# A decoder layer with expert retrieval on one core: steps traced later, the last gate's rows in their own buffers, and a final norm without GpSimd

## The chip, the cores and the metric

The kernel runs on one core of one Trainium2 chip. A core has a matrix engine (TensorE: PE in the profile, with PEld for its weight loads), a vector engine (VectorE: DVE), a scalar engine (ScalarE: ACT), GpSimd (POOL) and SyncE (SP). Each engine takes its own instructions strictly in the order in which they were issued, and waits at the head of its queue until the semaphores of that instruction are there. Transfers are issued from the queues of SP, ACT and POOL. The metric is device time in microseconds (us).

## What is computed

One decoder layer on 256 tokens of width 1024, in float32: a modulated norm, one input projection that feeds sparse attention and a short convolution, an output projection, a second modulated norm, an expert layer with 16384 experts of which each token picks 16 in each of 8 heads, and a final norm. The expert layer takes most of the time:

```python
def peer_ffn(xn, w_q, sub_keys, expert_u, expert_v):
    q = (xn @ w_q).reshape(B, S, PEER_HEADS, 2, PEER_QDIM // 2)
    s = jnp.einsum('bshpd,hpkd->bshpk', q, sub_keys)
    v_half, i_half = lax.top_k(s, PEER_TOPK)
    cand = v_half[..., 0, :, None] + v_half[..., 1, None, :]
    top_s, top_c = lax.top_k(cand.reshape(B, S, PEER_HEADS, PEER_TOPK * PEER_TOPK), PEER_TOPK)
    ...
    experts = i1 * PEER_NKEYS + i2
    g = jax.nn.softmax(top_s.astype(jnp.float32), axis=-1)
    ...
        u = expert_u[ec]
        act = jax.nn.gelu(jnp.einsum('cd,ced->ce', xc, u).astype(jnp.float32))
        return jnp.einsum('ce,ced->cd', gc * act, expert_v[ec])
# and in the layer: x = x + gt2 * peer_ffn(h2, ...); return rmsnorm(x, ln_final_g)
```

## The kernel before

The front part (norm, attention, convolution, output projection, second norm) ends at about 206 us of the span and is not touched. What follows is traced by hand: from L720 on the program is in manual order, so an engine's queue holds its instructions in the order in which the Python code traces them, and to "trace a step later" is to move it back in the queue of every engine that it uses.

**The first product.** All 128 tiles of `expert_u` (a tile is 128 experts x 1024) are multiplied with the 256 tokens. A weight tile is loaded on SP's queue into a ring of four buffers (`wraw`), ACT casts it to a high part (`whi`, L118), and the low part (`wlo`, L119) is a subtraction on GpSimd for tiles below `XL` and on VectorE from there on. `ahead` keeps three split tiles ready; `u_tile(i)` then issues 24 matmuls of 256 columns. ACT follows with the gelu.

- Tiles 0 to 27 (`XA` = 28, L1052): beside them VectorE finds the top experts (`topk`, a generator; each `yield` names an estimated cost, and a tile lets 2.2 us of it be traced). Its last step makes `keys` (L1007 to L1017), which TensorE transposes into `keyT` (L1066). The eight tiles of `w_mod` for the last gate go through the same `wraw` ring, one after every third u tile, and `last_gate` (L1030) adds each to `acc5` on VectorE.
- Tiles 28 to 61 (`XG` = 62, L1156): beside them the dense gate matrix is built: `gate.onehots` (VectorE, from `keyT`) and `gate.products` (16 short matmuls for 8 tokens).
- Tiles 62 to 127 (L1369): `make_list` finds which experts of which half of the tokens are used (`find_used`, 16 steps), numbers them, and in `list_part` makes two lists of row numbers, 8 columns at a time: three operations on VectorE (`oneR`, `oneQ`, half of `oneT`), one on ACT (the other half of `oneT`, L1215), and 8 short matmuls, which are traced one chunk later. A tile lets 2.7 of the estimated cost be traced. Products are stored to memory (`rows`) by SP. As soon as the first list is there, `pick` gathers activation rows with an indirect transfer from GpSimd's queue, up to 48 of them (`NA`) before the loop ends. At tile 100 (`XM`) `gate_rows` makes the last gate's rows: two scalings on VectorE, matmuls, additions, all traced at once.

**The second product** (L1438). For each of 95 listed columns of 128 experts, GpSimd gathers a tile of `expert_v` (128 x 1024) and, if it wasn't done before, the activation rows; `split_acts` (L1407) splits the activations (`ah` on ACT, `al` on VectorE), `next_weights` splits a weight tile two columns ahead, and TensorE adds 12 matmuls of 512 columns (both halves of the tokens) or 6 (one half). In ACT's and VectorE's queues the split of the activations of column n+1 stands behind the split of the weights of column n+2. There are as many v tiles in flight as seven buffers allow, and `pick` is called at a rate of 0.6 for each column until all 95 are picked.

**The end** (`tail`, L1511): residual, mean of squares, norm and output; GpSimd multiplies three halves of rows by the norm's gain.

Of the kernel before, what the change touches and what calls it, by code (L numbers as in the profile page):

```python
# [30 lines left out]
XL = 92  # L31
# [25 lines left out]
def layer(nc, tc, d, dbg=None):  # L57
# [37 lines left out]
    def mod_tile(j, k):  # L95
        return d["w_mod"][k * 128:(k + 1) * 128, j * D:(j + 1) * D]
# [769 lines left out]
    nmod = [0]  # L866
# [45 lines left out]
    def topk():  # L912
# [94 lines left out]
        ei = k.tile([128, 3, T], I32, name="ei")  # L1007
        V.tensor_copy(ei[:, 0], eid.rearrange("p t j -> p (t j)"))
        V.tensor_scalar(ei[:, 1], ei[:, 0], 7, None, op0=OP.logical_shift_right)
        V.tensor_scalar(ei[:, 2], ei[:, 0], 127, None, op0=OP.bitwise_and)  # L1010
        two = lambda ap: ap.unsqueeze(2).to_broadcast([128, T, 2])
        for n in range(2):
            V.tensor_copy(keys[:, n], two(ei[:, 1 + n]))
        ws = k.tile([128, T], F32, name="ws")
# [13 lines left out]
    acc5 = k.tile([128, D], F32, name="acc5")  # L1028

    def last_gate(raw):  # L1030
        gather_mod(acc5, raw, nmod[0])
        nmod[0] += 1
        if nmod[0] == KT_:
            Q.dma_start(acc5d, acc5)
# [8 lines left out]
    steps = topk()  # L1043
    for h, _ in enumerate(queries()):
        if h == H:
            S.activation(Ba[:, 0], u_tile(0), AF.Gelu_apprx_tanh)
        if h > 1:
            next(steps)
            next(steps)
            next(steps)  # L1050
    show("sco", sco)
    for i in range(1, XA):  # L1052
        S.activation(Ba[:, i], u_tile(i), AF.Gelu_apprx_tanh)  # L1053
        credit[0] += FREE
        while credit[0] > 0:
            credit[0] -= next(steps, 9.0)
# [3 lines left out]
    bs.close()  # L1060
    kt = pool("pskey", space=PSUM, stack=us)
# [140 lines left out]
    def list_part(p, work, pl, e1, e0, e, q0, n):  # L1202


        last = None
        for c0 in list(range(e0, e, 8)) + [None]:
            if c0 is not None:
                w = min(8, e - c0)
                cs = slice(c0, c0 + w)
                r = work.tile([128, 8, 128], F16, name="oneR", bufs=2)  # L1210
                paired(r[:, :w], io1, w, pl[0][:, cs], OP.is_equal)
                q = work.tile([128, 8, n], F16, name="oneQ%d" % n, tag="oneQ", bufs=1)
                paired(q[:, :w], io1[:, q0:q0 + n], w, pl[1][:, cs], OP.is_equal)
                t = work.tile([128, 8, 2, n], F16, name="oneT%d" % n, tag="oneT", bufs=2)
# [3 lines left out]
            if last:  # L1218
                l0, lw_, r0, t0 = last
                for c in range(lw_):  # L1220
                    mm(p, r0[:, c], t0[:, c].rearrange("p k q -> p (k q)"), l0 + c == e0, l0 + c == e - 1)
            last = c0 is not None and (c0, w, r, t)
# [10 lines left out]
    def make_list():  # L1233
# [21 lines left out]
        cs = lw.tile([NL, 3, 128], F16, name="cs")  # L1255
# [12 lines left out]
        t = lw.tile([128, 3, NL], F32, name="t3", tag="t3")  # L1268
        V.tensor_tensor(t, pos, m, op=OP.mult)
        un = lw.tile([128, NL], F32, name="un")  # L1270
# [6 lines left out]
        pi = lw.tile([128, 3, NL], I32, name="pi", tag="t3")  # L1277
# [36 lines left out]
    def gate_rows(acc5, out):  # L1314

        V.tensor_scalar(out, out, 1.0 / GSC, None, op0=OP.mult)
        V.tensor_scalar(acc5, acc5, 1.0 / GSC, None, op0=OP.mult)
        for n in range(2):
            cs = slice(n * 512, n * 512 + 512)
            p = keyT[n].rearrange("p a t -> p (a t)")  # L1320
            mm(p, ones, acc5[:, cs], True, True)
            V.tensor_add(out[:, cs], p, out[:, cs])
# [45 lines left out]
    log = []  # L1368
    for i in range(XG, NE):  # L1369
        gelu_tile(i)  # L1370
# [7 lines left out]
        if i == XM:  # L1378
            gate_rows(acc5, g2)
# [3 lines left out]
        credit[0] += 2.7  # L1383
# [7 lines left out]
    print("picks from", log[:1], "picked", len(picked), "stored", stored[0], "lists", ready_lists)  # L1391
# [3 lines left out]
    settle()  # L1395
    store_rows(NL)
# [31 lines left out]

    for i in range(NL, NE):
        acts = split_acts(Bb[:, i - XA], slice(0, T))  # L1430
        w = next_weights()
        for a in range(2):
            out_tile(acts, w, a)
# [4 lines left out]
    for n, q in enumerate(taken):  # L1438
        while later and len(taken) - len(later) < n0 + 2 + (n + 1) * 6 // 10:
            pick()  # L1440
        if n == 40:
            Q.dma_start(x1, x1d)
            row_bias(2, lnf)
            S.preload_act_table_set("natural_log_exp_and_others")
        t, halves = picked.pop(q), halves_of(q)
        acts = split_acts(t, columns(halves))
# [64 lines left out]
    def tail(fin):  # L1511
# [6 lines left out]
        G.tensor_mul(y[:, 0, 512:], x1[:, 0, 512:], lnf[:, 512:])  # L1518
# [6 lines left out]
        G.tensor_mul(y[:, 1, :512], x1[:, 1, :512], lnf[:, :512])  # L1525
# [17 lines left out]
        S.activation(y[:, 0, 512:], y[:, 0, 512:], AF.Copy, scale=r0)  # L1543
        store(0, Q, 512, 1024)
# [88 lines left out]
```

## Time and profile before

| | us |
|---|---|
| three runs before | 940.42, 942.26, 935.8 (median 940.42) |
| the profiled execution's own time | 935.07 |
| its span, first to last instruction | 933.1 |
| TensorE busy | 844.1 |
| VectorE busy | 672.2 |
| ScalarE busy | 471.7 |
| GpSimd busy | 514.8 |

The difference of 2.0 us between the execution's time and its span lies around the program. Busy times overlap. A row of the timeline gives the start, the duration, the engine and the line, and in brackets how long the engine had been idle and what ended that. A group of a view by line gives the busy time and the mean of one. The granted clock is TensorE's, as a share of its full speed.

### The profile page before, as it was taken

To read this page: it belongs to the slowest core of one execution; us is meant where nothing else is said; L and a number is where in the kernel's file an instruction comes from. 1 tells how busy PE (TensorE), PEld (TensorE's weight loads), DVE (VectorE), ACT (ScalarE), POOL (GpSimd) and SP (SyncE) were. 2 spreads that over 40 slices of the span, in tenths; PEclk is the share of its full clock that TensorE was granted. 3 is DMA by queue.
4 is the path that set the end of the run, shared out by engine and by line. 5 is a ranking of instruction groups with operands and counts; after the bars stand their busy time and mean duration, and the time that the engine had idled before them with its cause. 6 is when DMAs were issued, how large, how long until landed. Compare 5 with 4: busy or idle time off the path is not lost.

```text
span 933.1 us, 16274 instructions
## 1 busy us (share of the span) xinstructions
PE 844.1 (90%) x5954; PEld 744.5 (80%) x5954; DVE 672.2 (72%) x1553; ACT 471.7 (51%) x912; POOL 514.8 (55%) x324
## 2 busy tenths in 40 slices
PE   3599979989988989999999996999999999999992
PEld 2498868779988979999999996899976666666661
DVE  4747897678999988879799566555565556665565
ACT  3345866455534435555544364344445555555553
POOL 0002653431866846666687667751157888888731
PEclk8599998989989999999999999999999999999997
DMA  8898657135646734444489788998877777777761
GB/s 320 265 234 312 219 189 243 65 109 166 207 166 205 247 114 139 141 151 137 137 252 304 214 253 302 328 328 283 267 265 241 234 231 234 243 241 221 250 225 50
DMA packets 71204, 203.73 MB, mean 218 GB/s; under 512 B 8203, under 2 KB 25964, under 8 KB 70860
## 3 DMA queue, kind: packets, MB, share of 16 engines
q1 hardware_dynamic: 51776, 138.38, 45.4%
q0 software_dynamic: 18240, 62.27, 20.6%
q10 hardware_dynamic: 1100, 1.95, 0.6%
q8 instruction: 49, 0.80, 0.3%
q14 instruction: 39, 0.32, 0.1%
HBM read 183.11 MB, written 19.46 MB: 217 GB/s over the span
## 4 chain that ended last, share of the span: by engine, by line
PE 42%; DVE 23%; issue 11%; POOL 10%; DMA 8%; ACT 4%; SPq 0%; ACTq 0%; POOLq 0%; DVEq 0%
PE ps L74 24%; PE pj L74 7%; POOL Bb L84 5%; DVE used L1199 4%; POOL wraw L84 4%; PE pg L74 3%; DVE wlo L119 2%; DMA wraw<-w_mod 2%; PE sc L74 2%; ACT whi L118 2%; DMA Ba<-v,ixv 2%; PE pt L74 1%; PE acc L74 1%; DMA mraw<-w_mod 1%; DMA wraw<-v,ixv 1%
## 5 line engine op out<-in xcount | busy, mean ns | idle before, releaser
L119 POOL TENSOR_TENSOR wlo<-wraw,whi 128x1024 fp32r<-128x1024 f32 x101 | 245.3, 2432 | 232.0 <-ACT whi L118 224.6
L74 PE MATMUL ps<-hhi,whi 128*128 128x256 f32 x1024 | 297.7, 291 | 6.1 <-DVE eq L1001 2.9
L74 PE MATMUL ps<-hhi,wlo 128*128 128x256 f32 x1024 | 292.1, 285 | 2.5 <-POOL wlo L119 2.5
L74 PE MATMUL ps<-hlo,whi 128*128 128x256 f32 x1024 | 292.2, 285 | 0.0
L118 ACT CAST whi<-wraw 128x1024 fp32r<-128x1024 f32 (+1 forms) x218 | 226.1, 1038 | 109.9 <-PE acc L74 49.2
L119 DVE TENSOR_TENSOR wlo<-wraw,whi 128x1024 fp32r<-128x1024 f32 (+1 forms) x118 | 149.5, 1268 | 114.7 <-ACT whi L118 114.3
L74 PEld LDWEIGHTS ps<-hhi,whi 128*128 128x128 f32 x1024 | 197.0, 192 | 7.7 <-ACT Ba L1053 5.6
L74 PEld LDWEIGHTS ps<-hhi,wlo 128*128 128x128 f32 x1024 | 196.8, 192 | 3.0 <-POOL wlo L119 3.0
L74 PEld LDWEIGHTS ps<-hlo,whi 128*128 128x128 f32 x1024 | 197.0, 192 | 0.2 <-issue 0.2
L84 POOL DMA_INDIRECT Bb<-rows,ixact x75 | 91.1, 1215 | 22.9 <-issue 21.7
L74 PE MATMUL acc<-whi,ah 128*128 128x512 f32 x294 | 97.3, 410 | 5.4 <-ACT ah L1410 2.9
L74 PE MATMUL acc<-whi,al 128*128 128x512 f32 x294 | 97.3, 410 | 4.8 <-DVE al L1411 1.0
L74 PE MATMUL acc<-wlo,ah 128*128 128x512 f32 x294 | 92.9, 395 | 0.0
L84 POOL DMA_INDIRECT wraw<-v,ixv x53 | 64.5, 1218 | 43.1 <-DMA wraw<-v 22.7
L1147 ACT ACTIVATE ps<-ps 128x256 f32<-128x256 f32 (+16 forms) x99 | 33.0, 333 | 101.4 <-PE ps L74 98.8
L74 PEld LDWEIGHTS acc<-whi,ah 128*128 128x128 f32 x294 | 51.8, 188 | 33.6 <-ACT ah L1410 24.7
L74 PEld LDWEIGHTS acc<-whi,al 128*128 128x128 f32 x294 | 51.8, 188 | 33.6 <-DVE al L1411 24.6
L74 PEld LDWEIGHTS acc<-wlo,ah 128*128 128x128 f32 x294 | 55.4, 188 | 12.9
L369 POOL TENSOR_TENSOR macc<-macc,mraw 128x1024 f32<-128x1024 f32 x14 | 36.2, 2585 | 39.0 <-ACT mraw L368 32.0
L119 DVE TENSOR_TENSOR wlo<-Bb,whi 128x1024 fp32r<-128x1024 f32 x28 | 34.3, 1225 | 27.5 <-ACT whi L118 27.5
L1087 DVE TENSOR_TENSOR o<-io,keyT 128x1024 f16<-128x1024 f16 x64 | 41.1, 683 | 15.3 <-PE pg L74 15.3
L84 POOL DMA_INDIRECT Bb<-v,ixv x28 | 32.8, 1172 | 34.8 <-DVE Bb L1373 24.0
(364 smaller groups left out, 1474.7 us busy)
## 6 DMA issues: line engine op xcount, KB each, us to landing
wraw<-ut SPq DMA_DIRECT2D x128, 512.0 KB, 4.3
wraw<-w_mod SPq DMA_DIRECT2D x24, 512.0 KB, 4.6
mraw<-w_mod SPq DMA_DIRECT2D x24, 512.0 KB, 4.4
wraw<-win SPq DMA_DIRECT2D x20, 512.0 KB, 5.1
wraw<-w_out SPq DMA_DIRECT2D x8, 512.0 KB, 4.6
wraw<-wq SPq DMA_DIRECT2D x8, 512.0 KB, 3.6
rows<-Bb SPq DMA_DIRECT2D x6, 640.0 KB, 5.5
rows<-Bb SPq DMA_DIRECT2D x10, 384.0 KB, 5.8
```

Of the source, the lines that this page charges most:

```text
L74: E.matmul(out, lhsT, rhs, start=start, stop=stop)
L84: G.indirect_dma_start(out=out, out_offset=None, in_=rows, in_offset=bass.IndirectOffsetOnAxis(ap=ix, axis=0))
L118: in_order(S.copy(hi, raw))
L119: in_order(low.tensor_sub(lo, raw, hi.bitcast(F32)))
L369: G.tensor_add(accs[j], accs[j], w)
L1087: V.tensor_tensor(out.rearrange("p n (m b) -> p n m b", b=2), a, doubled(b).unsqueeze(2).to_broadcast(sh), op=op)
L1147: S.activation(p[:, :n], p[:, :n], AF.Gelu_apprx_tanh)
L1199: V.tensor_reduce(used[:, :, e:e + b.shape[1]].rearrange("p a e -> p e a"), b.rearrange("p e (a t) -> p e a t", a=2), axis=AX, op=OP.max, ...
```

## The change

1. **Top experts.** The step that copies `cid` on ACT is traced one step later; `keys` is made through tiles in PSUM (`ei0`, `ei`, `ws`) where it went through SBUF. The u tile 28 is traced ahead of the transposes of `keys`.
2. **Last gate.** The eight `w_mod` tiles leave the `wraw` ring for two buffers of their own (`raw5`), loaded on SP's queue at tiles -2, 1, 4, ... 19 and added on VectorE at tiles 3, 6, ... 24. `gate_rows` is cut into steps, one for each tile, begun when both lists are there.
3. **Lists.** In `list_part` the operation on ACT is traced one chunk after VectorE's, and the matmuls one chunk after that; tiles have more buffers and share tags. The cost that a tile lets be traced is 2.5 up to tile 92 and 1.3 from there on (it was 2.7); `XL` goes from 92 to 96.
4. **Second product.** The activations are split three columns ahead, before the weights; the picks run at n0 + 4 + 0.65 (n + 1), n0 being the number picked before (it was n0 + 2 + 0.6 (n + 1)). The ACT table for the end is loaded before the second product (it was at column 40).
5. **The end.** GpSimd's multiplications go; VectorE does the gain and the norm in one operation (`scalar_tensor_tensor`).

```diff
-XL = 92
+XL = 96
@@ order of the weight tiles
     for i in range(NE):
         put(d["ut"][i], low=G if i < XL else V)
-        if i < 3 * KT_ and i % 3 == 2:
-            put(mod_tile(5, i // 3), D, use=lambda raw: last_gate(raw))
@@ topk
+        yield 2.60
         for a in range(2):
             S.copy(cidp[a], cid[:, a * 8:a * 8 + 8])
-        yield 2.60
+        yield 0.50
...
-        ei = k.tile([128, 3, T], I32, name="ei")
-        V.tensor_copy(ei[:, 0], eid.rearrange("p t j -> p (t j)"))
...
+        ei0 = kps.tile([128, T], I32, name="ei0", tag="pk", bufs=2)
+        ei = kps.tile([128, 2, T], I32, name="ei", tag="pq", bufs=2)
+        V.tensor_copy(ei0, eid.rearrange("p t j -> p (t j)"))
+        V.tensor_scalar(ei[:, 0], ei0, 7, None, op0=OP.logical_shift_right)
+        V.tensor_scalar(ei[:, 1], ei0, 127, None, op0=OP.bitwise_and)
...
-        ws = k.tile([128, T], F32, name="ws")
+        ws = kps.tile([128, T], F32, name="ws", tag="pk", bufs=2)
@@ last gate
+    def last_gate(i):
+        n, r = divmod(i + 5, 3)
+        if r == 0 and n - 1 < KT_:
+            raw5.append(k.tile([128, D], F32, name="raw5", bufs=2))
+            Q.dma_start(raw5[-1], mod_tile(5, n - 1))
+        n, r = divmod(i, 3)
+        if r == 0 and 0 < n <= KT_:
+            gather_mod(acc5, raw5[n - 1], n - 1)
+            if n == KT_:
+                Q.dma_start(acc5d, acc5)
...
+    first = u_tile(XA)
     kt = pool("pskey", space=PSUM, stack=us)
...
-        p = u_tile(i)
+        p = first if i == XA else u_tile(i)
@@ list_part
+                paired(t[:, :w, 0], q[:, :w], w, e1[:, cs], OP.mult)
+                chunks.append((c0, w, r, q, t))
+            if 0 <= n_ - 1 < len(starts):
+                _, w, _, q, t = chunks[n_ - 1]
                 S.activation(t[:, :w, 1], q[:, :w], AF.Copy, scale=e2)
-                paired(t[:, :w, 0], q[:, :w], w, e1[:, cs], OP.mult)
-                yield 1.7
...
+            if n_ >= 2:
+                l0, w, r, _, t = chunks[n_ - 2]
+                for c in range(w):
+                    mm(p, r[:, c], t[:, c].rearrange("p k q -> p (k q)"), l0 + c == e0, l0 + c == e - 1)
+            yield 1.5
@@ the loop over tiles 62 to 127
-        if i == XM:
-            gate_rows(acc5, g2)
+            gated = gate_rows(acc5, g2)
+            next(gated)
+        if i >= XM and len(ready_lists) == 2:
+            next(gated, None)
...
-        credit[0] += 2.7
+        credit[0] += 2.5 if i + 3 < XL else 1.3
@@ the second product
+    def next_acts():
+        while sources and len(split_ahead) < 3:
+            t, halves = sources.pop(0)
+            split_ahead.append((split_acts(picked.pop(t) if isinstance(t, int) else t, columns(halves)), halves))
+        return split_ahead.pop(0)
+
+    S.preload_act_table_set("natural_log_exp_and_others")
...
-        while later and len(taken) - len(later) < n0 + 2 + (n + 1) * 6 // 10:
+        while later and len(taken) - len(later) < n0 + 4 + (n + 1) * 13 // 20:
...
-        acts = split_acts(t, columns(halves))
+        acts, halves = next_acts()
         w = next_weights()
@@ tail
-        G.tensor_mul(y[:, 0, :512], x1[:, 0, :512], lnf[:, :512])
...
+        V.tensor_mul(y[:, 1, :512], x1[:, 1, :512], lnf[:, :512])
...
-        V.tensor_mul(y[:, 1, 512:], x1[:, 1, 512:], lnf[:, 512:])
+        next(nrm)
+        V.scalar_tensor_tensor(y[:, 0], x1[:, 0], r0, lnf, op0=OP.mult, op1=OP.mult)
+        store(0, Q, 0, 1024)
         run(nrm)
-        S.activation(y[:, 1, :384], y[:, 1, :384], AF.Copy, scale=r1)
-        store(1, Q, 0, 384)
-        V.tensor_scalar(y[:, 1, 384:], y[:, 1, 384:], r1, None, op0=OP.mult)
-        store(1, S, 384, 1024)
+        S.activation(y[:, 1, :512], y[:, 1, :512], AF.Copy, scale=r1)
+        store(1, Q, 0, 512)
+        V.scalar_tensor_tensor(y[:, 1, 512:], x1[:, 1, 512:], r1, lnf[:, 512:], op0=OP.mult, op1=OP.mult)
+        store(1, S, 512, 1024)
```

## Rows read from the trace of the kernel before

**Rows 1.** Busy time of each engine in stretches of the span (start and end in us; then the length, and busy time with the number of instructions for PE, PEld, DVE, ACT, POOL; then granted clock, busy share of the DMA engines, GB/s).
```profile
234.10:327.60 93.50, 85.68 (x682) 84.31 (x680) 90.66 (x354) 42.81 (x66) 68.77 (x29) 0.95 0.61 206
...
333.50:459.80 126.30, 126.30 (x1306) 124.72 (x1306) 107.19 (x283) 69.48 (x160) 76.77 (x32) 0.99 0.41 132
...
556.00:597.50 41.50, 34.30 (x308) 33.77 (x307) 26.48 (x53) 17.43 (x28) 30.87 (x30) 0.96 0.92 317
...
603.50:678.10 74.60, 74.60 (x630) 74.51 (x628) 40.37 (x53) 34.34 (x52) 21.80 (x20) 1.00 0.90 293
...
715.00:884.00 169.00, 162.57 (x624) 111.57 (x623) 102.03 (x139) 92.25 (x141) 136.69 (x107) 1.00 0.75 235
```

**Rows 2.** Timeline of VectorE where `keys` is made and after (start, duration; then line, operation, output <- inputs).
```profile
290.43 0.42 DVE L976 CAST tpf<-tp 128x256 f32<-128x256 uint32 x1
...
324.29 1.45 DVE L1008 CAST ei<-eid 128x256 int32<-128x256 f32 x1
...
326.19 2.94 DVE L1013 CAST keys<-ei 128x512 f16<-128x512 int32 x2
329.05 2.43 DVE L1015 TENSOR_SCALAR ws<-w 128x256 f32<-128x256 f32 x1
...
331.97 0.69 DVE L1017 TENSOR_TENSOR keys<-ws,keys 128x512 f16<-128x512 f32 x1
332.58 1.28 DVE L1087 TENSOR_TENSOR o<-io,keyT 128x1024 f16<-128x1024 f16 x2
333.96 1.28 DVE L1087 TENSOR_TENSOR gw<-o,keyT 128x1024 f16<-128x1024 f16 x2
```

**Rows 3.** Timeline of GpSimd in the same stretch.
```profile
323.20 2.39 POOL L119 TENSOR_TENSOR wlo<-wraw,whi 128x1024 fp32r<-128x1024 f32 x1 [0.26 <-ACT whi L118]
326.05 2.45 POOL L119 TENSOR_TENSOR wlo<-wraw,whi 128x1024 fp32r<-128x1024 f32 x1 [0.46 <-ACT whi L118]
328.89 2.43 POOL L119 TENSOR_TENSOR wlo<-wraw,whi 128x1024 fp32r<-128x1024 f32 x1 [0.40 <-ACT whi L118]
```

**Rows 4.** The two casts of `keys` by themselves: number, shortest, median and longest duration in ns.
```profile
L1013 DVE CAST keys<-ei x2: 415/1508/2602, 326.2 to 328.7; 128x512 f16<-128x512 int32 x2
```

**Rows 5.** Timeline of TensorE from the transposes of `keys` to the first products of the gate (the bracket is its idle time).
```profile
328.94 0.69 PE L1066 MATMUL keyT<-ident,keys 128*128 128x128 f32 x4 [1.48 <-DVE keys L1013]
...
333.06 0.56 PE L74 MATMUL ps<-hhi,whi 128*128 128x256 f32 x1
...
337.16 1.07 PE L74 MATMUL pg<-gw,o 128*128 128x128 f16 x16
```

**Rows 6.** Who waited for whom from 234 to 333.5 us (engine, line, released by; total us, times, longest).
```profile
ACT whi L118 <- DMA wraw<-ut: 11.5, 4, 6.2
...
ACT cid L990 <- DVE cid L984: 3.8, 1, 3.8
```

**Rows 7.** Who waited for whom from 533.6 to 603.5 us, where the lists and the last gate's rows are made.
```profile
PE numbers L74 <- ACT oneT L1215: 7.1, 4, 3.2
...
PE keyT L74 <- DVE Ba L1317: 1.3, 1, 1.3
```

**Rows 8.** Timeline of TensorE while the used experts are looked for: the first and the last of the three tiles before which it sat idle (from 455 to 515 us).
```profile
474.40 0.36 PE L74 MATMUL ps<-hhi,whi 128*128 128x256 f32 x1 [0.34 <-DVE Bb L1373]
...
506.93 0.36 PE L74 MATMUL ps<-hhi,whi 128*128 128x256 f32 x1 [0.19 <-DVE Bb L1373]
```

**Rows 9.** Timeline of GpSimd: the first gather of activations, the first gather of a v tile for the ring at the end of the first product, and the last gather of activations.
```profile
557.79 1.13 POOL L84 DMA_INDIRECT Ba<-rows,ixact  x1 [2.29 <-DVE ixact L1229]
...
673.06 0.94 POOL L84 DMA_INDIRECT wraw<-v,ixv  x1 [22.72 <-DMA wraw<-v]
...
878.80 1.92 POOL L84 DMA_INDIRECT Bb<-rows,ixact  x1 [0.30 <-issue]
```

**Rows 10.** GpSimd's gathers from 715 to 884 us (shortest, median, longest in ns) and the idle time before them.
```profile
L84 POOL DMA_INDIRECT Bb<-rows,ixact x39: 947/1180/1942, 716.9 to 878.8; - x39
...
  issue: 30.5, 100
```

**Rows 11.** Who waited for whom from 700 to 884 us.
```profile
ACT whi L118 <- PE acc L74: 73.2, 37, 2.2
...
PEld acc L74 <- ACT ah L1410: 19.6, 37, 1.9
```

**Rows 12.** Timeline of ACT over one pair of columns (one with 12 matmuls, one with 6): the cast of weights that opens the pair, and the one that opens the next.
```profile
725.39 1.05 ACT L118 CAST whi<-wraw 128x1024 fp32r<-128x1024 f32 x1 [2.22 <-PE acc L74]
...
730.25 1.05 ACT L118 CAST whi<-wraw 128x1024 fp32r<-128x1024 f32 x1 [2.21 <-PE acc L74]
```

**Rows 13.** Timeline of TensorE at the start of the second product, six matmuls apart, and its last matmul.
```profile
680.24 0.62 PE L74 MATMUL acc<-whi,al 128*128 128x512 f32 x2
...
681.63 0.64 PE L74 MATMUL acc<-whi,al 128*128 128x512 f32 x2
...
916.86 0.40 PE L74 MATMUL acc<-whi,al 128*128 128x512 f32 x1
```

**Rows 14.** Timeline of the end: VectorE, GpSimd, and ACT's last transfer.
```profile
916.20 1.17 DVE L1495 TENSOR_TENSOR Bb<-Bb,ft 128x512 f32<-128x512 f32 x1
...
915.53 1.29 POOL L1515 TENSOR_TENSOR Ba<-Bb 128x512 f32<-128x512 f32 x1 [16.59 <-DVE Bb L1495]
...
924.15 0.38 ACTq L1509 DMA_DIRECT2D out<-Ba  x1
```

More of the change, by code (lines that the diff above doesn't have):

```diff
@@ L1005, in topk @@
         show("w16", w)
[L1007 to L1010 removed]
+        ei0 = kps.tile([128, T], I32, name="ei0", tag="pk", bufs=2)
[3 more added lines that the diff above has]
+        V.tensor_scalar(ei[:, 1], ei0, 127, None, op0=OP.bitwise_and)
         two = lambda ap: ap.unsqueeze(2).to_broadcast([128, T, 2])
         for n in range(2):
[L1013 to L1014 removed]
+            V.tensor_copy(keys[:, n], two(ei[:, n]))
+        ws = kps.tile([128, T], F32, name="ws", tag="pk", bufs=2)
         V.tensor_scalar(ws, w.rearrange("p t j -> p (t j)"), GSC, None, op0=OP.mult)
@@ L1028, in layer @@
     acc5 = k.tile([128, D], F32, name="acc5")
[L1030 to L1034, printed above, removed]
+    raw5 = []
+    def last_gate(i):
[8 more added lines that the diff above has]
+                Q.dma_start(acc5d, acc5)
     rows = [dram.tile([(1 + e - e0) * 128, T], F32, name="rows%d" % e0) for e0, e, *_ in LISTS]
@@ L1202, in list_part @@
     def list_part(p, work, pl, e1, e0, e, q0, n):
-        last = None
-        for c0 in list(range(e0, e, 8)) + [None]:
-            if c0 is not None:
+        starts, chunks = list(range(e0, e, 8)), []
+        for n_ in range(len(starts) + 2):
+            if n_ < len(starts):
+                c0 = starts[n_]
                 w = min(8, e - c0)
                 cs = slice(c0, c0 + w)
-                r = work.tile([128, 8, 128], F16, name="oneR", bufs=2)
+                r = work.tile([128, 8, 128], F16, name="oneR", bufs=3)
                 paired(r[:, :w], io1, w, pl[0][:, cs], OP.is_equal)
-                q = work.tile([128, 8, n], F16, name="oneQ%d" % n, tag="oneQ", bufs=1)
+                q = work.tile([128, 8, n], F16, name="oneQ%d" % n, tag="oneQ", bufs=2)
                 paired(q[:, :w], io1[:, q0:q0 + n], w, pl[1][:, cs], OP.is_equal)
-                t = work.tile([128, 8, 2, n], F16, name="oneT%d" % n, tag="oneT", bufs=2)
-                S.activation(t[:, :w, 1], q[:, :w], AF.Copy, scale=e2)
-                paired(t[:, :w, 0], q[:, :w], w, e1[:, cs], OP.mult)
-                yield 1.7
[L1218 to L1222, printed above, removed]
+                t = work.tile([128, 8, 2, n], F16, name="oneT%d" % n, tag="oneT", bufs=3)
+                paired(t[:, :w, 0], q[:, :w], w, e1[:, cs], OP.mult)
+                chunks.append((c0, w, r, q, t))
+            if 0 <= n_ - 1 < len(starts):
+                _, w, _, q, t = chunks[n_ - 1]
+                S.activation(t[:, :w, 1], q[:, :w], AF.Copy, scale=e2)
+            if n_ >= 2:
[3 more added lines that the diff above has]
+            yield 1.5
     def row_numbers(p, e0, q0, work, n):
@@ L1254, in make_list @@
             mm(sums[:, c], m[:, c], one16, True, True)
-        cs = lw.tile([NL, 3, 128], F16, name="cs")
+        cs = lw.tile([NL, 3, 128], F16, name="cs", tag="oneR", bufs=3)
         V.tensor_copy(cs, sums)
@@ L1267, in make_list @@
                 mm(ends[:, c], cs[:, b], same[:NL, 0, 0:NL:LISTS[1][0]], b == 0, b == c)
-        t = lw.tile([128, 3, NL], F32, name="t3", tag="t3")
+        t = lw.tile([128, 3, NL], F32, name="t3", tag="oneR", bufs=3)
         V.tensor_tensor(t, pos, m, op=OP.mult)
-        un = lw.tile([128, NL], F32, name="un")
+        un = lw.tile([128, NL], F32, name="un", tag="oneR", bufs=3)
         V.tensor_tensor(un, f[:, 0], m[:, 2], op=OP.add)
@@ L1276, in make_list @@
         V.tensor_scalar(un[:, e0:], un[:, e0:], 128.0 * e0, None, op0=OP.add)
-        pi = lw.tile([128, 3, NL], I32, name="pi", tag="t3")
+        pi = lw.tile([128, 3, NL], I32, name="pi", tag="oneR", bufs=3)
         V.tensor_copy(pi[:, 0], un)
@@ L1309, in make_list @@
             ready_lists.append(e0)
+            log.append(-i_[0])
     stored = [0]
     def gate_rows(acc5, out):
+        yield
         V.tensor_scalar(out, out, 1.0 / GSC, None, op0=OP.mult)
         V.tensor_scalar(acc5, acc5, 1.0 / GSC, None, op0=OP.mult)
-        for n in range(2):
-            cs = slice(n * 512, n * 512 + 512)
-            p = keyT[n].rearrange("p a t -> p (a t)")
+        yield
+        parts_ = [(keyT[n].rearrange("p a t -> p (a t)"), slice(n * 512, n * 512 + 512)) for n in range(2)]
+        for p, cs in parts_:
             mm(p, ones, acc5[:, cs], True, True)
+        yield
+        for p, cs in parts_:
             V.tensor_add(out[:, cs], p, out[:, cs])
@@ L1367, in layer @@
     credit[0] = 0.0
-    log = []
+    log, i_ = [], [0]
     for i in range(XG, NE):
+        i_[0] = i
         gelu_tile(i)
@@ L1390, in layer @@
                     pick()
-    print("picks from", log[:1], "picked", len(picked), "stored", stored[0], "lists", ready_lists)
+    print("picks from", [x for x in log if x<0],[x for x in log if x>0][:1], "picked", len(picked), "stored", stored[0], "lists", ready_lists)
     assert len(ready_lists) == 2
@@ L1395, in layer @@
     settle()
+    for _ in gated:
+        pass
     store_rows(NL)
@@ L1427, in halves_of @@
         return [a for a, (q0, q1) in enumerate(((0, n0), (m0, m1))) if q0 <= q - e0 < q1]
+    sources = [(Bb[:, i - XA], [0, 1]) for i in range(NL, NE)] + [(q, halves_of(q)) for q in taken]
+    split_ahead = []
+    def next_acts():
[4 more added lines that the diff above has]
+    S.preload_act_table_set("natural_log_exp_and_others")
     for i in range(NL, NE):
-        acts = split_acts(Bb[:, i - XA], slice(0, T))
+        acts, _ = next_acts()
         w = next_weights()
```

11 lines of the change are left out of this document (2 added, 9 removed).

## The prediction

> **What bounds the kernel now.** The busy time of the engines by stretch comes first, because no engine is full over the whole span. I call tiles 0 to 27 stage A, tiles 28 to 61 B, tiles 62 to 127 C, the second product D. The late part of C, where TensorE never stops, gives a u tile's price: 74.6 us for 630 matmuls, 24 a tile, is 2.84 us [rows 1]. B is full of matmuls, 126.3 of 126.3 us, so only its start can move. In A the 28 tiles need 28 x 2.84 = 79.5 of 93.5 us while VectorE is busy for 90.66: VectorE's top-expert chain sets the end of A. Where the lists are made TensorE works 34.30 of 41.5 us. From 715 to 884 us GpSimd runs 107 gathers in 136.69 us, and before each stand 30.5 / 100 = 0.305 us of issue [rows 1, 10]: 136.7 + 32.6 = 169.3 of 169 us, so it is full.
>
> Then the waits. TensorE waits 7.1 us for ACT's half of the lists and 1.3 us for the scaled gate rows [rows 7]. In D ACT waits 73.2 us for TensorE and TensorE's weight loads 19.6 us for ACT's `ah` [rows 11]. That is a loop: a cast of weights waits for a free buffer, and the next column's `ah` stands behind it. A pair of columns takes 730.25 - 725.39 = 4.86 us [rows 12]; its 18 matmuls would take 3 x 1.39 = 4.17 us [rows 13]. So D has two limits that lie close together, the loop (2.43 us a column) and GpSimd.
>
> **Stage A.** From L1008 to the first `o` VectorE spends 332.58 - 324.29 = 8.29 us on eight small operations [rows 2]. L1008, one L1013 and L1015 end just after GpSimd's low parts do (325.59, 328.50, 331.32), so they wait for GpSimd [rows 2, 3]; L1013 takes 0.415 us at best and 2.602 at worst [rows 4]. The changed ones go through PSUM. Nearest rows: a cast of 256 elements into PSUM took 0.42 us, one of 512 elements 0.69 while GpSimd was working [rows 2]; 4 x 0.42 + 4 x 0.69 = 4.4, a gain of 3.9 us. Bounds: nothing, if they still wait, and 5.
>
> The Trainium skill speaks against this edit (VectorE: DVE Perf Modes, "Why PSUM operands drop a tier"): with an operand in PSUM the doubled mode that uses both SBUF read ports is gone. The best L1013 against the 0.69 of L1017 agrees [rows 2, 4]; by that alone four operations would lose 1.1 us and the total below would be 5 us higher.
>
> With u tile 28 ahead of the transposes TensorE fills its wait there. Now products start 337.16 - 332.58 = 4.58 us after the keys, u tile 28 lying between at 4.10 us in place of 2.84, as it follows idle time [rows 5]. Then they wait for the transposes (0.69) and for `o` and `gw` (335.24 - 332.58 = 2.66): 3.35. That is 1.2 less, of which I take 0.6, because slow matmuls after the wait move to the gate and tile 29. A: -4.5, from 0 to -6.
>
> The `w_mod` tiles' own buffers remove part of the 11.5 us that ACT waits for weights, and the later `cid` copy 3.8 us [rows 6]. I cost both at nothing: VectorE's 90.66 busy us cover them. Without that cover TensorE's idle 93.5 - 85.68 = 7.8 us would be at stake [rows 1]. Each `raw5` load waits on SP's queue for the addition two before it, which is traced one tile earlier, and the u loads behind it wait too; six tiles are loaded or in flight then, and VectorE, which makes the keys of tile 26 at 324 us, is one or two tiles late.
>
> **Stage C.** With ACT's part traced a chunk later and matmuls another, the 7.1 us go [rows 7], except where two chunks fall into one tile: 2.5 / 1.5 of cost makes that three times in the first list, never in the second (1.3 / 1.5). There a gelu and ACT's part still stand before the second chunk's matmuls; I estimate 0.65 us each, 2.0 in all. -5.1. Gate rows cut into tiles: -1.3. Fewer used-steps a tile (2.5 / 2.3, was 2.7 / 2.3): the three short stalls, two of them 0.34 and 0.19 [rows 8], go: -0.9. C: -7.3, from -3 to -9.3. The list matmuls stay.
>
> The four low parts that move to GpSimd cost 4 x 2.4 = 9.6 us there [rows 3], and the first pick moves from tile 90 to 94. Behind them are the gathers of activations. GpSimd idles 22.7 us before 673 [rows 9], so time is covered; the count is not. By the loop's own arithmetic 45 rows are picked in place of 48, and ahead of the first v tile for the ring 41 in place of 47: six gathers move into D.
>
> **Stage D**, from the first ring gather at 673.06 [rows 9]. Now the last pick belongs to column 74 and comes after 128 gathers, at 880.7. With 0.65 a column it belongs to column 66; v tiles are then issued up to column 74: 72 + 54 = 126 gathers. An undisturbed one takes 0.947 + 0.305 = 1.25 us [rows 10]; the mean of 136.69 / 107 = 1.277 adds 0.33, or 107 x 0.33 / (169 / 2.43) = 0.51 us for each column: VectorE's subtractions hold gathers up. With a low part for each tile in C the same stretch is (30.87 - 30 x 0.947) / (41.5 / 2.84) = 0.17 a tile [rows 1]. After the change VectorE's blocks of four become blocks of two; I take 0.45, near D's own row, and keep 0.17 and 0.51 as bounds. 126 x 1.25 + 69 x 0.45 + 4 us of first waits = 192.5. TensorE is then three columns behind, at 72, and the other 23 columns (198 matmuls of 0.232) take 46 us, now without the loop: 238.5. Now it is 917.26 - 673.06 = 244.2 [rows 13]. D: -5.7, from -23 to -2; all 882 matmuls back to back from 679 would give -33. The earlier ACT table load takes place of one at column 40: 0.
>
> **The end.** VectorE no longer runs into GpSimd (L1495 takes 1.17 us under GpSimd's 1.29 [rows 14], where 512 elements take 0.69 [rows 2]): -0.9 with a second such case. The 1024-wide operation in front of the last small ones costs 2 x 0.69 = 1.4. +0.5, from -1 to +2; it ends at 924.15 now [rows 14].
>
> **Sum.** -4.5 - 7.3 - 5.7 + 0.5 = -17.0: the profiled 935.07 becomes 918.1. The median of the three runs is 5.3 us above the profiled one; I predict 920, between the two ways of counting.
>
> **Rivals.**
> - GpSimd takes D back: six more gathers, and a stretch of 0.6 a column, as more matmuls mean denser subtractions. 157.5 + 41.4 + 4 + 46 = 248.9, D +4.7; total -6.6: 928. For it: GpSimd is already full. Against: its own blocks get shorter. Chance 0.16.
> - The keys gain nothing, VectorE losing elsewhere what it gains, because its other operations then meet GpSimd: A -0.6, total -13: 922. Chance 0.13.
> - The stretch falls towards C's: at 0.2, D is 221, total -34: 901. For it: the C row; against: D has two subtractions a column. Chance 0.14.
> - Slower: every column's weight subtraction catches a gather in full. The longest gather took 1.942 - 0.947 = 1.0 us more than an undisturbed one [rows 10]; 157.5 + 69 + 4 + 46 = 276.5, D +32, total +21: 956. It decides above 0.45 + 17 / 69 = 0.70 a column. Against: the mean is 0.51 and most gathers take 0.95 to 1.2. Chance 0.07. The Trainium skill (SBUF — State Buffer, "SBUF: two separate sides") says that VectorE and GpSimd lock their shared ports for a whole instruction; the keys' rows look like that.
>
> The forecast has 0.50. Under 1% measurement can't tell a change of this kernel from none. Faster by over 1%: the forecast, the second and third rival, less what of them ends short: 0.75. Within 1%: the first rival and that remainder: 0.17. Slower: 0.08. The range holds the forecast, the third rival's 901 almost, and the first's 928 with the 5 us between profile and median: 902 to 933.
>
> **What would show it.** L1013 and L1015 near 0.7 and 0.4 us; TensorE's products 5 us earlier; TensorE waiting at most 2 us for ACT in the lists; 45 picks before the end of C; ACT's wait for TensorE in D no longer between pairs but GpSimd still full to the last pick, near 0.45 of stretch a column, and pairs of 4.2 us after it. The forecast fails if the stretch is far from 0.45, or if a new wait stands at the head of VectorE's or SP's queue in A.

## The result and the profile after

The changed kernel takes 910.9 us (median of 4 runs, 904.1 to 913.5), the kernel before 939.8 in runs on the same chip: ratio 0.9685, interval 0.9622 to 0.9748. The forecast was 920, range 902 to 933. Four of the experiments below (e5 to e8) ran on a chip on which the kernel before took 990 us; their ratios are against that.

The stages can be measured in the same way in every trace: by the starts of ACT's activations of u tiles 0, 40, 62 and 127, the end of the last matmul and the start of the last store. The stages are the prediction's, but A here goes on to tile 40. Worked out from the timelines, in us:

| kernel | to tile 0 | A: 0 to 40 | B: 40 to 62 | C: 62 to 127 | D: to the last matmul | to the last store | to the span's end | span |
|---|---|---|---|---|---|---|---|---|
| before | 237.4 | 146.2 | 82.1 | 212.7 | 239.0 | 6.9 | 9.0 | 933.1 |
| after | 242.3 | 145.1 | 82.0 | 199.1 | 228.0 | 7.3 | 5.8 | 909.6 |
| difference | +4.9 | -1.0 | 0.0 | -13.5 | -11.0 | +0.4 | -3.2 | -23.5 |

The first column is noise: but for one load of 512 KB (`raw5`) no edit touches what runs there, and over the 14 traces of this study it lies between 236.9 and 245.8, with the old code (236.9 to 243.5) as with the new. Without it the difference is 28.4 us, which is that of the medians (28.9).

Busy time by stretch after the change (columns as in [rows 1]): stage A, the stretch in which the lists end, late C, and D while picks last.

```profile
239.00:332.50 93.50, 83.98 (x685) 83.25 (x684) 92.09 (x352) 42.58 (x66) 71.34 (x29) 0.95 0.59 199
560.00:603.50 43.50, 43.50 (x405) 43.06 (x404) 29.10 (x53) 22.52 (x36) 34.40 (x27) 1.00 0.97 330
603.50:668.00 64.50, 64.50 (x536) 63.54 (x535) 37.17 (x53) 29.04 (x44) 27.64 (x25) 1.00 0.94 311
705.00:861.00 156.00, 146.15 (x599) 111.41 (x598) 98.06 (x134) 86.67 (x133) 123.73 (x106) 0.99 0.79 250
```

Against [rows 1]: A is as full of VectorE as it was (92.09 of 93.5); in the two stretches of C shown TensorE is busy all the time; in D GpSimd makes 106 gathers in 156 us, 0.68 per us, where it made 107 in 169, 0.63.

VectorE where the keys are made (timeline; start, duration), beside [rows 2]:

```profile
331.65 0.43 DVE L1007 CAST ei<-eid 128x256 int32<-128x256 f32 x1
332.12 0.43 DVE L1008 TENSOR_SCALAR ei<-ei 128x256 int32<-128x256 int32 x1
332.58 0.43 DVE L1009 TENSOR_SCALAR ei<-ei 128x256 int32<-128x256 int32 x1
333.05 1.29 DVE L1012 CAST keys<-ei 128x512 f16<-128x512 int32 x2
334.26 0.42 DVE L1014 TENSOR_SCALAR ws<-w 128x256 f32<-128x256 f32 x1
334.71 0.69 DVE L1015 CAST keys<-ws 128x512 f16<-128x512 f32 x1
335.43 0.69 DVE L1016 TENSOR_TENSOR keys<-ws,keys 128x512 f16<-128x512 f32 x1
336.94 1.29 DVE L1097 TENSOR_TENSOR o<-io,keyT 128x1024 f16<-128x1024 f16 x2 [0.81 <-PE keyT L1076]
```

No operation is stretched any more: the eight operations end 4.47 us after the first one's start, and the first operation of the gate (`o`) starts 5.29 us after it, in place of 8.29. Between them VectorE now waits 0.81 us for the transposes of `keys`. TensorE, after the change and in e4, where the keys are made in SBUF again:

```profile
336.27 1.06 PE L1076 MATMUL keyT<-ident,keys 128*128 128x128 f32 x8 [1.11 <-DVE keys L1016]
```

```profile
335.81 0.69 PE L1075 MATMUL keyT<-ident,keys 128*128 128x128 f32 x4 [1.42 <-DVE keys L1011]
```

With the keys in SBUF four of the eight transposes run before the last key operations, as they did before the change [rows 5]; with their tiles in PSUM all eight come after the last one. What holds the first four back was not tested.

Earlier in the same chain three operations of 0.28 and 0.29 us now last 2.4 to 2.5 (VectorE's groups of stage A, each shape apart: after, then the same operations before):

```profile
L946 DVE TENSOR_TENSOR cand<-tv 128x128 f32<-128x128 f32 x1 | 2.5, 2486 | 0.0
L953 DVE TENSOR_TENSOR cand<-tv 128x128 f32<-128x128 f32 x1 | 2.5, 2484 | 0.0
...
L939 DVE TENSOR_SCALAR ixf<-ixf 128x256 f32<-128x256 f32 x1 | 2.4, 2367 | 0.0
```

```profile
L942 DVE TENSOR_SCALAR ixf<-ixf 128x256 f32<-128x256 f32 x1 | 0.3, 294 | 0.0
...
L949 DVE TENSOR_TENSOR cand<-tv 128x128 f32<-128x128 f32 x1 | 0.3, 280 | 0.0
L956 DVE TENSOR_TENSOR cand<-tv 128x128 f32<-128x128 f32 x1 | 0.3, 279 | 0.0
```

Each of the three ends about 0.15 us after a low part of GpSimd (270.46 after 270.31, 275.40 after 275.26, 278.39 after 278.24): the meeting of [rows 2, 3], in another place. In the other direction two operations of before (the first of 64 elements in L949, 2.42 us, and L966, 2.38) are down to 0.22 and 0.40. Together these five cost 2.3 us more than before, which takes back most of the 3.0 us that the chain gains where the keys are made.

Who waited for whom after the change: C to the end of the lists (463 to 603.5 us), beside [rows 7] and [rows 8]; then ACT and TensorE in D (705 to 861 us), beside [rows 11].

```profile
PE numbers L74 <- ACT oneT L1230: 1.9, 3, 0.6
...
PEld L74 <- DVE m L1262: 1.1, 1, 1.1
PE sums L74 <- DVE m L1262: 1.0, 1, 1.0
...
PE ps L74 <- DVE Bb L1391: 0.3, 1, 0.3
```

```profile
ACT whi L118 <- PE acc L74: 24.0, 16, 1.5
ACT whi L118 <- DMA wraw<-v,ixv: 22.0, 18, 2.1
...
ACT whi L118 <- DMA Bb<-v,ixv: 11.0, 9, 1.6
...
ACT whi L118 <- DMA Ba<-v,ixv: 7.6, 6, 2.6
```

ACT's wait for TensorE fell from 73.2 us (in 184 us) to 24.0 (in 156); 40.6 us of waits for gathered v tiles stand in its place. The loop no longer sets the pace; the gathered tiles come late.

### The profile page after: what moved, and what is told of

It reads as the page before. It is cut to its first block, busy times and chain, and to the rows that moved or that the text cites. A ratio compares the mean times of both kernels' runs of the same rounds, so it can differ in the third digit from the quotient of the medians.

```text
span 909.6 us, 16292 instructions
## 1 busy us (share of the span) xinstructions
PE 828.8 (91%) x5954; PEld 750.2 (82%) x5954; DVE 669.9 (74%) x1549; ACT 470.4 (52%) x911; POOL 515.6 (57%) x325
## 4 chain that ended last, share of the span: by engine, by line
PE 44%; DVE 22%; issue 12%; DMA 11%; POOL 8%; ACT 2%; SPq 0%; ACTq 0%; POOLq 0%; DVEq 0%
PE ps L74 25%; PE pj L74 6%; DMA wraw<-v,ixv 6%; POOL Bb L84 4%; DVE used L1209 4%; PE pg L74 3%; POOL wraw L84 2%; PE acc L74 2%; PE pt L74 2%; DMA wraw<-w_mod 2%; DVE acc L247 1%; DVE wlo L119 1%; DMA Ba<-v,ixv 1%; PE sc L74 1%; DVE tm L925 1%
## 5 line engine op out<-in xcount | busy, mean ns | idle before, releaser
L119 POOL TENSOR_TENSOR wlo<-wraw,whi 128x1024 fp32r<-128x1024 f32 x105 | 256.0, 2441 | 225.7 <-ACT whi L118 212.9
L119 DVE TENSOR_TENSOR wlo<-wraw,whi 128x1024 fp32r<-128x1024 f32 (+1 forms) x114 | 140.7, 1236 | 91.8 <-ACT whi L118 88.5
L74 PE MATMUL acc<-wlo,ah 128*128 128x512 f32 x294 | 95.5, 404 | 6.5 <-DVE wlo L119 6.4
L74 PE MATMUL acc<-whi,ah 128*128 128x512 f32 x294 | 94.6, 401 | 6.5 <-ACT whi L118 4.2
L84 POOL DMA_INDIRECT Bb<-rows,ixact x75 | 85.5, 1141 | 22.9 <-issue 19.8
L74 PE MATMUL acc<-whi,al 128*128 128x512 f32 x294 | 94.2, 400 | 0.0
L74 PEld LDWEIGHTS acc<-whi,ah 128*128 128x128 f32 x294 | 55.4, 191 | 22.8 <-ACT whi L118 7.8
L74 PEld LDWEIGHTS acc<-whi,al 128*128 128x128 f32 x294 | 56.2, 191 | 13.2
L74 PE MATMUL pj<-hhi,whi 128*128 128x256 f32 x160 | 49.7, 312 | 1.2 <-ACT Y L403 0.5
```

Source lines behind the costliest of these rows:

```text
L74: E.matmul(out, lhsT, rhs, start=start, stop=stop)
L84: G.indirect_dma_start(out=out, out_offset=None, in_=rows, in_offset=bass.IndirectOffsetOnAxis(ap=ix, axis=0))
L119: in_order(low.tensor_sub(lo, raw, hi.bitcast(F32)))
```

## The experiments

Stages of each, as in the first table, then the median time of its runs and its ratio to the kernel before on the same chip:

| run | A | C | D | us | ratio (interval) |
|---|---|---|---|---|---|
| e1 | 145.1 | 198.1 | 244.7 | 920.6 | 0.982 (0.977 to 0.987) |
| e2 | 145.4 | 199.1 | 210.0 | 887.4 | 0.946 (0.941 to 0.951) |
| e3 | 145.2 | 196.4 | 222.9 | 902.8 | 0.961 (0.955 to 0.967) |
| e4 | 146.5 | 197.9 | 221.8 | 907.4 | 0.968 (0.962 to 0.974) |
| e5 | 147.0 | 256.2 | 237.0 | 979.3 | 0.991 (0.987 to 0.994) |
| e6 | 146.7 | 238.9 | 242.2 | 973.4 | 0.988 (0.980 to 0.997) |
| e7 | 145.3 | 251.1 | 238.9 | 971.3 | 0.983 (0.977 to 0.989) |
| e8 | 145.3 | 244.8 | 240.6 | 965.5 | 0.977 (0.968 to 0.985) |
| e9 | 145.3 | 196.4 | 224.7 | 901.6 | 0.959 (0.956 to 0.963) |
| e10 | 146.8 | 214.2 | 217.9 | 917.5 | 0.976 (0.971 to 0.981) |
| e11 | 146.3 | 199.3 | 239.0 | 926.3 | 0.985 (0.979 to 0.990) |
| e12 | 145.6 | 197.7 | 209.0 | 891.0 | 0.951 (0.948 to 0.955) |

The code of D is the same in the changed kernel, e3 and e4, and D took 228.0, 222.9 and 221.8: differences of D below some 6 us say nothing.

**e1: the order of the splits undone** (and with it the table load back at column 40).

```diff
...
-        acts, halves = next_acts()
+        t, halves = picked.pop(q), halves_of(q)
+        acts = split_acts(t, columns(halves))
```

> The changed kernel with only the order of the activations' split undone: a column's high part is cast when the column is reached, not three columns ahead. Theory 1 (the loop of ACT and TensorE set D together with GpSimd): ACT's wait for TensorE returns to about 70 us in D, the second product takes about 238 us again from the last activation of the first product to its last matmul (228 with the change, 239 before), total about 921. Theory 2 (GpSimd's gathers alone set D, the gain came from fewer and shorter ones): D stays within 3 us of 228, total 909 to 914.

D went to 244.7, the total to 920.6: theory 1. ACT's wait for TensorE came back in part (700 to 861 us), beside waits for gathers, so both limits are there at once:

```profile
ACT whi L118 <- PE acc L74: 42.6, 24, 3.2
ACT whi L118 <- DMA wraw<-v,ixv: 22.0, 16, 2.3
```

The 5.7 us over the 239.0 of the kernel before lie within the noise of D.

**e2: no gathers of activations in D.**

```diff
-        gather(t[:, 0], rows[list_of(q)], lists["act"][:, q:q + 1])
+        if direct[0]:
+            Q.dma_start(t[:, 0], rows[list_of(q)][128:256])
+        else:
+            gather(t[:, 0], rows[list_of(q)], lists["act"][:, q:q + 1])
...
-    n0 = len(picked)
+    n0, direct[0] = len(picked), True
```

> The changed kernel in which the picks of the second product read a fixed block of rows with a plain transfer on SP's queue in place of GpSimd's gather (the same bytes, the wrong expert's activations, so the output is not the reference's): 50 gathers less for GpSimd in D. Theory 1 (GpSimd is the bound of D after the change): its 50 x 1.47 us go, D falls from 228 us to TensorE's own 206 to 212, total 890 to 896. Theory 2 (the transfers themselves or ACT set D): D stays above 222, total above 905.

Theory 1, and 3 us below its lower end (887.4). Busy time from 700 to 850 us, and what ended GpSimd's idle time before its gathers there:

```profile
700.00:850.00 150.00, 150.00 (x647) 121.60 (x647) 106.89 (x146) 93.69 (x145) 71.26 (x73) 1.00 0.80 265
```

```profile
  DVE wlo L119: 52.9, 32
  DVE al L1436: 25.4, 34
```

TensorE is full, GpSimd waits for buffers; 210 us is about what TensorE itself needs. The changed kernel has some 12 to 18 us above that.

**e3: the lists as before**, under the changed pace: `list_part` as in the kernel before (but for one more buffer of `oneR`).

```diff
...
+                S.activation(t[:, :w, 1], q[:, :w], AF.Copy, scale=e2)
+                paired(t[:, :w, 0], q[:, :w], w, e1[:, cs], OP.mult)
+                yield 1.7
...
```

> The changed kernel with only the lists made as before (ACT's part and VectorE's in one step, TensorE's matmuls in the next). Theory 1 (the wait for ACT and the slow clock that follows each wait were the gain of C): TensorE's wait for ACT's part goes from 1.9 to 7 us or more, the granted clock from 1.00 to 0.96 there, C is 9 to 11 us longer, total about 920. Theory 2 (only the wait itself counts): C is 5 us longer, total about 916. Theory 3 (the finer credit carries the lists whatever their order): C within 2 us, total 911 to 913.

Theories 1 and 2 fell, and theory 3 did not go far enough: without the new order C is 196.4, shorter than in the four undisturbed traces that have it (197.9 to 199.1). From 535 to 605 us TensorE is busy for 69.41 of 70 us and never waits for ACT:

```profile
535.00:605.00 70.00, 69.41 (x655) 68.50 (x654) 43.79 (x91) 37.10 (x61) 53.37 (x40) 1.00 0.91 308
```

The 1.9 us that are left after the change come with the new order: the four undisturbed traces that have it (after, e1, e2, e4) show this wait at 1.9 us, the four with the new pace and the old order (e3, e9, e11, e12) show none. The length of C itself, 196.4 to 199.3 in those four, doesn't tell the orders apart.

**e4: the keys back in SBUF.** The tiles `ei` and `ws` as in the kernel before.

> The changed kernel with only the keys' intermediate tiles back in SBUF. Theory 1 (in PSUM the small operations don't meet GpSimd, and this is worth its face value): the eight operations take about 8.3 us to the first operation of the gate, as before the change, in place of 5.3; stage A ends 3 us later, total about 914. Theory 2 (a meeting avoided here only falls on another operation, as the profile after the change shows on two index operations of 2.4 us): total 910 to 912, with the eight operations between 4 and 8 us and other operations faster than with the change by as much.

```profile
330.64 1.98 DVE L1006 CAST ei<-eid 128x256 int32<-128x256 f32 x1
332.66 0.30 DVE L1007 TENSOR_SCALAR ei<-ei 128x256 int32<-128x256 int32 x1
332.87 0.29 DVE L1008 TENSOR_SCALAR ei<-ei 128x256 int32<-128x256 int32 x1
333.07 2.93 DVE L1011 CAST keys<-ei 128x512 f16<-128x512 int32 x2
335.92 0.28 DVE L1013 TENSOR_SCALAR ws<-w 128x256 f32<-128x256 f32 x1
336.24 0.43 DVE L1014 CAST keys<-ws 128x512 f16<-128x512 f32 x1
```

From the first to `o` it takes 6.67 us: two meetings with GpSimd in place of three. A is 146.5, inside the 146.2 to 147.0 of the five traces with the old stage A; with keys in PSUM it is 145.1 to 145.6 in eight. So the keys in PSUM are worth 1.2 us, the 0.81 us of new wait included, and all else that the change does in A nothing together. Neither theory has its total (907.4 lies below both). The 6.67 us are within theory 2's 4 to 8, but the operations of 2.4 us earlier in the chain are there in e4 too; they belong to where the chain now lies beside GpSimd, not to the keys.

**e5 and e10: the order of the splits alone**, in the kernel before (`next_acts` and the table load, nothing else).

> The kernel before with only the activations' splits traced three columns ahead (and ACT's table loaded ahead of D); lists, rate and number of the picks, keys and end as before. Theory 1 (the order of the splits is the whole gain of D): D falls from 239 to 220 to 225 us, total 920 to 925. Theory 2 (the faster rate of picks is needed for it, since the last pick stays at column 74): D falls by less than 8 us, total above 929.

> The same kernel as e5, once more for the same reason: the kernel before with only the activations' splits three columns ahead. Theory 1 (the order of the splits is the whole gain of D): D 220 to 225 us, total 920 to 925. Theory 2 (the faster rate of picks is needed for it): D falls by less than 8 us from 239, total above 929.

In e10 D is 217.9, 21 us less than before; total 917.5. Theory 1, and 2 us below its range: the order of the splits gives the gain by itself, without the faster rate of picks. D is also less than in the changed kernel (228.0, and 221.8 in e4), and a column is faster (2.11 us against 2.26, see e12), which points to another edit of D that takes some of it back. In e5, D is 237.0: the pauses of the last section lie in its D too. Busy time of e10 from 718 to 872 us:

```profile
718.00:872.00 154.00, 150.11 (x630) 116.83 (x629) 102.55 (x141) 90.45 (x140) 121.42 (x107) 1.00 0.81 262
```

**e6 and e11: the pace of the lists alone**, in the kernel before. The second list then ends later, so the last gate's rows are made at tile 112.

```diff
-XM = 100
+XM = 112
-        credit[0] += 2.7
+        credit[0] += 2.5 if i + 3 < XL else 1.3
```

> The kernel before with only the pace of the lists' steps changed (2.5 a tile, then 1.3 from tile 89, in place of 2.7; the last gate's rows at tile 112 in place of 100, since the second list then ends at tile 110). Theory 1 (the second list was too dense, two chunks in one tile; the pace alone takes the wait away): TensorE's wait for ACT falls from 7.1 to under 1 us and C from 212.7 to 198 to 202; 43 picks in place of 48 cost D up to 8 us; total 925 to 933. Theory 2 (ACT's part has to be traced later, too): the wait stays at 4 us or more, C 207 or longer, total 935 to 943.

> The same kernel as e6, once more for the same reason: the kernel before with only the slower pace of the lists' steps. Theory 1 (the pace alone takes the wait for ACT away): no such wait, C 198 to 202 where before has 212.7; 43 picks in place of 48 cost D up to 8 us; total 925 to 933. Theory 2 (the order is needed too): C 207 or longer, total 935 to 943.

In e11 C is 199.3, with no wait for ACT's part and none for the gate rows, and the total 926.3: theory 1. While the lists are made TensorE is full (537 to 607 us):

```profile
537.00:607.00 70.00, 70.00 (x649) 69.21 (x647) 45.34 (x86) 36.18 (x58) 39.65 (x31) 1.00 0.90 290
```

e6 has no such wait either. And D took 239.0 with 145 gathers from the first v tile gathered into the ring (`wraw`) to the last pick, where before has 128: 17 more gathers cost nothing.

**e8: the old end.** The last norm as in the kernel before.

> The changed kernel with only the last norm as before (GpSimd multiplies, five stores). Theory 1 (the 3.2 us between the last store's start and the end of the span belong to the way the end is stored): from the last matmul to the last store 6.9 us in place of 7.3, and 9 us from there to the end of the span in place of 5.8: total 2.8 us longer, 911 to 914. Theory 2 (they belong to something else): 5.8 us stay, total 908 to 911.

From the last store to the span's end it is 9.0 us again: theory 1 in that sum. To the last store it is 7.2, where theory 1 had 6.9. Its whole time can't be set against the changed kernel's, which did not run on that chip. The last store, of e8 (span 966.5) and after (span 909.6):

```profile
957.48 0.37 ACTq L1540 DMA_DIRECT2D out<-Ba  x1
```

```profile
903.83 0.35 ACTq L1540 DMA_DIRECT2D out<-Ba  x1
```

In all six traces with the old end the span ends 12.4 to 12.6 us after GpSimd's last multiply, and that lies 3.5 us before the last store. Whether GpSimd's late work or the fourth store makes the 3.2 us was not separated.

**e7 and e9: e3, with all 48 picks ahead of the first ring gather.**

```diff
-            for _ in range(1 + (i % 3 == 0)):
+            for _ in range(2):
```

> The changed kernel with the lists made as before (which ran at 902.8 us) and two picks in each tile of C in place of one or two: all 48 picks stand ahead of the first gather into the ring in place of 43. Theory 1 (GpSimd's count of gathers sets D): 5 gathers of 1.45 us less in D, total 894 to 898. Theory 2 (more gathers in C hold up VectorE and the transfers of u tiles, and D's slack is elsewhere): C longer by 2 us or more, total 902 or more.

> The same kernel as e7, once more, because in the four runs of e5 to e8 all engines stood still some 40 us in C for nothing that the profile shows. The changed kernel with the lists made as before (902.8 us in e3) and all 48 picks ahead of the first gather into the ring, in place of 43. Theory 1 (GpSimd's count of gathers sets D): 122 gathers in place of 128 up to the last pick, D 216 to 219 us where e3 had 222.9, total 894 to 899. Theory 2 (gathers moved into C cost there what they save in D): C 199 or longer, total 901 or more.

Theory 1 fell in e9: D stayed at 224.7 though 122 gathers stand before the last pick in place of 128, and that pick ends 10 us earlier than after the change. Theory 2 has the total (901.6) but not its cause, as C stayed at 196.4. The time can't be told from e3's. The 4 to 7 us that theory 1 asked for are about the noise of D, so e9 alone doesn't rule it out. Neither e9, with 6 gathers fewer, nor e11, with 17 more, shows an effect of their number up to the last pick.

**e12: e9 with the picks of D spread.**

```diff
-        while later and len(taken) - len(later) < n0 + 4 + (n + 1) * 13 // 20:
+        while later and len(taken) - len(later) < n0 + 4 + (n + 1) // 2:
```

> The kernel of e9 (the changed one with the lists made as before and two picks a tile) with the picks of D spread: one every second column in place of 13 in 20. Theory 1 (what counts in D is how many gathers stand against one column while picks last: 1.65 x 1.49 us = 2.46 us of GpSimd a column is over TensorE's 2.1, 1.5 x 1.45 = 2.18 hardly): columns 10 to 60 take 2.08 to 2.15 us each (2.25 in e9, 2.11 in e10 at 12 in 20), D 211 to 217 us, total 888 to 895. Theory 2 (the last pick, now at column 84 or so, becomes late, as in the kernel before with its last pick at column 74): D 222 or longer, total 900 or more.

Theory 1, with D 2 us below its range: D 209.0, as short as in e2, with all 95 picks still made, at 891.0 us 4.9% below the kernel before. Of the versions that compute the layer it is the fastest here. From 700 to 860 us TensorE is busy throughout, and ACT waits for it alone:

```profile
700.00:860.00 160.00, 160.00 (x690) 129.75 (x689) 111.20 (x155) 100.55 (x155) 124.66 (x114) 1.00 0.86 280
```

```profile
ACT whi L118 <- PE acc L74: 58.4, 38, 1.5
```

Columns 10 to 60 (starts of the casts of weights) take 2.06 us each; 2.25 in e9, 2.26 after, 2.11 in e10, 2.40 before. D is 15.7 us shorter than in e9, in one trace of each. The ratios to the kernel before differ by 0.8%, some 8 us, and the medians by 10.6; e9's trace is that of the longest of its seven runs (909.7 us). So the rate of the picks is worth 8 to 16 us.

## Why the prediction came out as it did

The direction and the range held; the sum of -17.0 was 28. All four parts of the sum were off by 3 to 6 us, and luck helped: the gain of A was taken 3.5 us too large, which hid part of the 14 us by which those of C, D and the end were too small. By its own steps:

- **Keys** (-3.9): the eight operations took 4.47 us against the 4.4 estimated, but A is 1.0 to 1.3 shorter, not 4.5. Two things were missing. VectorE waits 0.81 us for the transposes, a new wait at the head of its queue, which the prediction had named as a sign of failing. And the second rival, that VectorE meets GpSimd elsewhere, is what happened; its "A -0.6" was the better number. The 0.69 us for 512 elements was right by luck: the row that it was taken from (L1017) subtracts two operands in SBUF, and at 331.97 us no low part of GpSimd is running [rows 3], so it showed neither PSUM nor a meeting. Nor does it bear out the loss in PSUM; the rows after the change do, with 0.69 for the cast of `ws` (L1015) against 0.43 in e4. The Trainium skill (VectorE: DVE Perf Modes, "Why PSUM operands drop a tier") held for the undisturbed operations: a shift took 0.43 us in PSUM, 0.29 to 0.30 in SBUF (e4). **u tile 28 ahead** (-0.6): nothing beyond the keys can be seen; the slow matmuls moved to tile 29, as said (granted clock 0.66 from 342 to 345 us, between 1.00 and its lower level of 0.50). **`raw5`, `cid`** at nothing: right.
- **Lists** (-5.1): the size was right (7.1 to 1.9 us), the reason wrong. "With ACT's part traced a chunk later and matmuls another, the 7.1 us go": they go by the pace alone (e11, e3), the second list no longer having two chunks in a tile; the order costs those 1.9 us. **Gate rows** (-1.3): the size was right; in e11 the wait goes too, with the rows made late but all at once, so cutting them wasn't needed for it. **Used steps** (-0.9): 0.9 to 0.3.
- **What was left out of C**: it lost 13.5, not 7.3. TensorE's idle time fell by 9.2 (12.4 to 3.2): 1.8 more for `place` and 0.3 for `sums`, which the pace moved to other tiles. The other 4.4 are busy time. Before, the granted clock stood at 0.50, the lower of its two levels, in two stretches of C:

```profile
523.40:526.80 3.40, 3.40 (x18) 3.40 (x18) 1.37 (x11) 1.32 (x2) 1.88 (x1) 0.50 0.99 298
581.40:584.80 3.40, 2.95 (x17) 3.05 (x18) 2.07 (x6) 1.33 (x2) 2.79 (x3) 0.50 0.79 271
```

TensorE had been idle for 1.3 us up to 511 and 1.8 us up to 523 us ahead of the first, and for 1.6, 0.7, 1.6 and 3.2 us between 567 and 582 ahead of the second; behind its other waits in C the clock stayed at 1.00, and after the change it did so in all of C, with waits of up to 1.0 us. Half of 2 x 3.4 is 3.4 of the 4.4 us. So a stall can cost more than its length.
- **D** (-5.7, measured -11.0, and -16 to -17 in e3 and e4): the failed step is "so it is full". GpSimd's gathers plus their issue do fill its time, but they also do so at 0.71 gathers per us (e12: 124.66 + 35.2 of 160 us) where before had 0.63, so that sum is no proof of a bound. The loop alone set D: a column took 2.40 us from the tenth to the sixtieth and 2.40 in the last fifteen, nearly all behind the last pick at 878.80 [rows 9], and 17 more gathers moved nothing (e11). The casts that open and close those fifteen, before:

```profile
875.37 1.05 ACT L118 CAST whi<-Bb 128x1024 fp32r<-128x1024 f32 x1 [1.01 <-PE acc L74]
...
911.41 1.05 ACT L118 CAST whi<-wraw 128x1024 fp32r<-128x1024 f32 x1 [0.16 <-PE acc L74]
```

The loop's price is 21 us (e10). Then the model of the changed D, a stretch of 0.45 for each column up to the last pick at 126 gathers, was too high in the one (0.35 measured: (123.73 - 106 x 0.947) / 66.6 columns) and too low in the other (133 gathers; the last pick belongs to column 70, not 66: 66 follows from 48 picks ahead, 70 from the prediction's own count of 45). At 0.35 the measured stretch lies between the forecast's and the third rival's 0.2, and so do the gains. The gain that the faster rate of picks takes back (13 in 20: 1.65 gathers a column, at the 160 / 114 = 1.40 us of e12, are 2.31 us, over TensorE's 2.06) was not seen as such; the first rival, in which GpSimd takes back part of D, is nearest to it in kind, not in size. e12 shows its size: 8 to 16 us. That pairs take 4.2 us behind the last pick came out: 2.08 us a column in the last fifteen.
- **End** (+0.5): +0.4 to the last store. The 3.2 us behind it were not foreseen.

## What to carry to other kernels

Two limits that look equally full are told apart by a stretch in which one is absent: the columns after the last pick ran at the same 2.40 us, and that was in the trace before. When a producer on another engine is traced later, ask how its work is spread as well as where it stands: here the pace of the lists was worth 13 us and their order nothing; in D the order of the splits was worth 21 us and the rate of the picks 8 to 16, and the number of gathers up to the last pick showed no effect (e9, e11). A short operation that is stretched by another engine may be cured in one place and reappear in the same chain, so such a gain is counted over the whole chain.

## What the runs showed of the hardware that was not expected

- In e5 to e8 TensorE paused again and again in C, in e8 for up to 2.5 us at a time, for nothing that the profile shows, ACT for even longer. Who waited in e8 from 560 to 625 us:

```profile
ACT ps L1157 <- remote: 35.6, 1, 35.6
PEld ps L74 <- issue: 28.1, 23, 2.5
...
PE ps L74 <- issue: 26.7, 20, 2.4
```

All four had it, and no other trace (C 239 to 256 us against 196 to 214). D was disturbed as well: in e5, e7 and e8 ACT's casts of weights wait 10.6 to 17.6 us for `remote` there. The kernel before took 990 us on that chip, 50 more than elsewhere, but no trace of it was kept there. The cause stays open.

- The same gather lasts differently in different surroundings: 1.25 us on average in the three kernels with the loop (before, e1, e11), 1.09 in e12, 0.98 in e2, where GpSimd waits for buffers. What holds it up was not separated.
